# A decoder block on one core: gate and up products ahead of down products, earlier exponentials, a sixth shared block, another order at the end

## The chip, the cores and the metric

The kernel runs on one core of a Trainium2 chip. The metric is device time in microseconds for one execution of the whole program; lower is better. Three runs of the kernel before gave 692.03, 692.99 and 694.44 us, so the median is 692.99.

## The reference

One layer over 256 tokens of width 1024, all in float32. Its parts, cut to what matters here:

```python
c_act = silu(c)
mod = c_act @ w_ada + b_ada                    # (1, 6 * 1024): six vectors
sh1, sc1, g1, sh2, sc2, g2 = split(mod, 6)
h = rmsnorm(x, norm1_g) * (1 + sc1) + sh1
...                                            # one input projection, two attention branches, gates
x = x + g1 * (merged @ w_out)
h2 = rmsnorm(x, norm2_g) * (1 + sc2) + sh2
# mixture of experts: best of 4 groups, best 2 of its 8 experts, 32 experts in all
g_w, g_idx = top_k(softmax(h2 @ w_group + b_group), 1)
e_w, e_idx = top_k(softmax(logits of that group), 2); e_w /= sum(e_w)
y = sum over the two picks of g_w * e_w * ((silu(h2 @ w_gate[e]) * (h2 @ w_up[e])) @ w_down[e])
x = x + g2 * y
out = rmsnorm(x, final_g)
```

The weights are some 257 MB, of which the 32 experts are 201 MB; each weight is read once.

## The kernel before, in words

**Memory and the order of loads.** On-chip memory is one arena, handed out by the program itself while it is written (`Arena`, first fit; `get` with `high` takes the top of the smallest region that fits). A list `order` (lines 187 to 207) holds every weight load in the order in which SP issues it: blocks of w_in and w_ada, the output projections, then for each expert its gate and up weights ("gu") and its down weights ("dn"). `feed()` (line 212) issues the next loads as long as the arena has room, after first serving the areas asked for by `want`. `done(u)` gives an area back and is followed by `feed()`. SP works in order, so a load that waits for its room holds every load behind it. Experts 0 to 4 are loaded in pieces of a quarter ("gu", four of them) and a half ("dn"), later experts whole.

**The order of work.** Inside a `manual_schedule` block the engines named run their instructions as written; outside it a scheduler orders each engine's instructions at build time, and may also put later ones into gaps of a manual block.

**The modulation.** The first two vectors of mod are made ahead of the rest; the other four are eight blocks of 512 columns, numbered 4 to 11, each from two loads. `ada_four(u)` (line 413) either multiplies all eight row groups on TensorE, four at a time in four column strips (line 424), or, for a block in SHARED, lets VectorE add up five of the eight row groups beforehand (`ada_step`, lines 404 to 411, called between the weight splits of the input projection that UNITS pairs the block with, line 547) and multiplies the remaining four on TensorE (line 419). Block 5 belongs to input projection 3 and block 8 to input projection 5.

**The chain to expert 0.** After the output projection the new x is normed and routed in a manual block (lines 947 to 1346): `route` finds group and experts, `places` counts the slots of each token, `first_hots` and `first_sums` gather the rows of expert 0, `gather_first` turns and modulates them (VectorE lines 1052 and 1061, TensorE line 1057), `one_hots` prepares the selection for experts 1 to 3. `first_rows` (line 1233) adds x to the result y in PSUM, where the experts' results are added too; three of its eight products stand inside the block (line 1332) and five behind it (lines 1376 and 1377).

**The experts.** For each expert `hidden(e)` (line 1141) multiplies the gathered rows by gate and up (line 1129 for experts 0 to 4, line 1151 after), and `swiglu` finishes on ScalarE and VectorE; `outputs(e)` (line 1159) multiplies by the down weights (line 1133). Every four experts form a batch: `gather` (line 1018) selects, turns and modulates 128 rows with TensorE (lines 1027 and 1031), and `combine` adds the batch to y. `pick_weights` (line 1243) makes the weights of the picks from the logits with exponentials. After `outputs(0)` come the five products of `first_rows`, the gather of experts 1 to 3 and `pick_weights`.

**The end.** Experts 28 to 31 are added to y one by one (`add`, line 1097: VectorE scales, TensorE adds, line 1104). Expert 31's products come before expert 30's down products, with three warm-up products (`warm`, line 327: bf16 products of a matrix of ones, whose result nobody reads) in the middle. Then `last_outputs` (line 1185) takes the squares of y on ScalarE (line 1216), multiplies y by the final weight on VectorE (`with_g`, line 1210), forms the norm (`power` and `newton`, lines 1198 to 1207) and scales and stores the result. [...]

Of the kernel before, what the change touches and what calls it, by code (L numbers as in the profile page):

```python
# [32 lines left out]
OV_AT = NE - 3  # L33
EXTRAS_AT = 2
UNITS = ((4, (4,)), (3, (5,)), (5, (8,)), (6, (9, 6)), (7, (7,)), (8, (10,)), (9, (11,)))
SHARED = (8, 9, 7, 10, 11)
DMA_SCRATCH = 1024

PLACES = {"x": 25, "xH": 24, "xL": 23, "xn": 22, "xT": 21, "hT": 20, "wsp0": 14,
# [77 lines left out]
def tile_block(ctx: ExitStack, tc: tile.TileContext, d, out):  # L117
# [822 lines left out]
    def places(t):  # L940
# [3 lines left out]
            te.matmul(pos[:, t, :], oneb, mt[:, 0, :], start=False, stop=False)  # L944
        te.matmul(pos[:, t, :], trib, mt[:, t, :], start=False, stop=True)

    chain = ExitStack()
    chain.enter_context(tc.manual_schedule(engines={mybir.EngineType.PE, mybir.EngineType.DVE,
                                                    mybir.EngineType.Activation, mybir.EngineType.Pool}))
# [40 lines left out]
    class Batch:  # L990
# [106 lines left out]
        def add(self, i, dn):  # L1097

            q = self.dq[:, 256 * i:256 * i + 256]
            ve.tensor_tensor(q, dn[:, 0:256], g2g[0], op=OP.mult)  # L1100
            for t in range(2):
                for j in range(4):
                    r = slice(32 * j, 32 * j + 32)
                    te.matmul(y[j // 2][:, j % 2, t, :], self.pt4[r, i, 128 * t:128 * t + 128], q[r, :],  # L1104
                              start=False, stop=i == 3, skip_group_check=True)
# [79 lines left out]
    def last_outputs(hq, b):  # L1185

        e = NE - 1
        m3, ss3 = rt([2], "m3"), rt([2, 2], "ss3")
        q3, u3, r3 = rt([2], "q3"), rt([2], "u3"), rt([2], "r3")
        dn = wk(f"dn{e}")  # L1190
        for i, (k0, n) in enumerate(LAST):
            w = got[("dn", e, i)]
            for k in range(n):
                down(dn, hq, w[:, k, :], k0 + k)
        b.add(3, dn)
        halves = [slice(512 * n, 512 * n + 512) for n in range(2)]

        def power(t):

            i = slice(t, t + 1)  # L1200
            ve.scalar_tensor_tensor(m3[:, i], ss3[:, t, 0:1], EPS * D, ss3[:, t, 1:2], op0=OP.add, op1=OP.add)  # L1201
            gp.tensor_tensor(q3[:, i], m3[:, i], nhalf, op=OP.pow)  # L1202

        def newton(t):
            i = slice(t, t + 1)
            ve.scalar_tensor_tensor(u3[:, i], q3[:, i], m3[:, i], q3[:, i], op0=OP.mult, op1=OP.mult)  # L1206
            ve.scalar_tensor_tensor(r3[:, i], u3[:, i], -3.0, q3[:, i], op0=OP.add, op1=OP.mult)  # L1207

        def with_g(t, n):
            ve.tensor_tensor(v3(fo[:, t, halves[n]], 2), y[n][:, :, t, :], v3(fg[:, halves[n]], 2),  # L1210
                             op=OP.mult)


        for n in (1, 0):
            for t in range(2):
                sc.activation(v3(junk[:, 0:512], 2), y[n][:, :, t, :], AF.Square, accum_out=ss3[:, t, n:n + 1])  # L1216
        with_g(0, 0)
        with_g(1, 0)
        with_g(0, 1)
        power(0)  # L1220
        with_g(1, 1)
        power(1)
        newton(0)
        newton(1)
        for t, n in ((0, 0), (0, 1), (1, 0), (1, 1)):
            o = fo[:, t, halves[n]]
            if t == 1:
                ve.tensor_scalar(o, o, r3[:, t:t + 1], None, op0=OP.mult)  # L1228
            else:
                sc.activation(o, o, AF.Copy, scale=r3[:, t:t + 1])  # L1230
            sp.dma_start(out[0, 128 * t:128 * t + 128, halves[n]], o)

    def first_rows(t, js):
        for j in js:
            te.matmul(y[j // 2][:, j % 2, t, :], ident, x_sb[:, t, 256 * j:256 * j + 256],
                      start=t == 0, stop=False, skip_group_check=True)


    wts = rt([2, 2], "wts")
    gw = rt([2, 1], "gw")  # L1240
    nmx = rt([2, 1], "nmx")

    def pick_weights():
        ve.tensor_scalar(nmx, g8[:, :, 0:1], -1.0, None, op0=OP.mult)
        for t in range(2):
            sc.activation(rt([4], f"gx{t}"), lg[:, t, 0:4], AF.Exp, bias=nmx[:, t, :], accum_out=gw[:, t, :])
        ve.tensor_tensor(wts[:, :, 1:2], v8[:, :, 1:2], v8[:, :, 0:1], op=OP.subtract)
        sc.activation(wts[:, :, 1:2], wts[:, :, 1:2], AF.Exp)
        ve.scalar_tensor_tensor(wts[:, :, 0:1], wts[:, :, 1:2], 1.0, gw, op0=OP.add, op1=OP.mult)
        ve.reciprocal(wts[:, :, 0:1], wts[:, :, 0:1])  # L1250
        ve.tensor_tensor(wts[:, :, 1:2], wts[:, :, 1:2], wts[:, :, 0:1], op=OP.mult)

# [79 lines left out]
    p = wk("xr0")  # L1334
    cur.first_sums(p, 0)
    places(1)
    cur.first_hots(1)
    cur.first_sums(p, 1)
    cur.gather_first(p, modr)
# [3 lines left out]
                                    op0=OP.is_equal, op1=OP.mult, accum_out=ms[:, t, i:i + 1])  # L1343
    cur.one_hots(slice(0, 128))
    cur.ready = 128
    chain.close()
    nxt = None
    for e in range(NE):
        if e % 4 == 0 and e >= 4:
# [5 lines left out]
        if e == NE - 4:  # L1355
# [8 lines left out]
                              start=True, stop=True, skip_group_check=True)  # L1364
                ve.tensor_scalar(fg[:, 512 * n:512 * n + 512], q, -16.0, None, op0=OP.mult)
            cur.weights()
        hq = hidden(e, cur)
        if e == NE - 2:
            with tc.manual_schedule(engines={mybir.EngineType.PE, mybir.EngineType.DVE, mybir.EngineType.Activation}):
                hq, hl = hidden(NE - 1, cur), hq  # L1370
                outputs(e, cur, hl)
                last_outputs(hq, cur)
            break
        outputs(e, cur, hq)
        if e == 0:
            first_rows(0, (3,))
            first_rows(1, range(4))
            cur.gather(slice(32, 128))
            pick_weights()
        if e == 4:  # L1380
            overflow_rows()
        if e % 4 == 0 and e < NE - 4:
# [38 lines left out]
```

## Time and profile before

| | |
|---|---|
| runs | 694.44, 692.03, 692.99 us; median 692.99 |
| profiled execution | 694.41 us; span from first to last instruction 692.6 us |
| mean granted TensorE clock | 0.918 of full speed |
| TensorE busy | 543.2 us, 78% |
| VectorE busy | 297.5 us, 43% |
| ScalarE busy | 157.7 us, 23% |
| DMA | 259.26 MB, mean 374 GB/s over the span |

Times in the profile count from the first instruction. Busy time is an average over stages with different limits, so the table alone doesn't say what bounds the kernel: the slices of the page, the timelines and the windows below do. In a timeline a row gives start and duration in us, engine, line, operation, tile written <- tiles read, shape and count, and in brackets the idle time before it and what ended it. [...]

### The profile page before, as it was taken

The page shows a single profiled execution, that of the slowest core. Times are in us where ns is not written, and L with a number is a line of the kernel's source. Part 1 is how long each engine was busy: PE and PEld are TensorE (multiplying, and loading weights), DVE is VectorE, ACT ScalarE, POOL GpSimd, SP SyncE. Part 2 cuts the span into 40 slices and gives each one's busy share as a digit, 9 for nine tenths or more (in the row PEclk, how much of TensorE's full clock was granted, in tenths as well). Part 3 has the DMA queues.
Part 4 walks back from the last instruction along what each step waited for, and adds up shares of the span by engine and source line. Part 5 has one row for each costly group of instructions (what it writes and reads, how often), then busy time and mean ns, then how long its engine had stood idle before and what let it go on. Part 6 is the DMA issues. An engine that isn't in the chain of part 4 may idle for free. (4 is left out here: it accounts for less than half of the span.)

```text
span 692.6 us, 14947 instructions
## 1 busy us (share of the span) xinstructions
PE 543.2 (78%) x6499; PEld 379.8 (55%) x6499; DVE 297.5 (43%) x840; ACT 157.7 (23%) x350; POOL 6.7 (1%) x21
## 2 busy tenths in 40 slices
PE   8999999999999997878848647656855755686572
PEld 4667766666788744556635435434544444365451
DVE  5359977858787466454314213121421211221012
ACT  3345755575554321001000000000000000010002
POOL 1000000000000000000000000000000000000000
PEclk9999999999999999999988989976998998799775
DMA  9999979649986989999999999999999999999971
GB/s 316 365 374 386 387 253 387 223 155 387 409 324 225 341 297 399 427 429 423 428 427 423 427 429 424 425 428 427 425 428 427 424 424 429 426 425 428 425 308 61
DMA packets 53965, 259.26 MB, mean 374 GB/s; under 512 B 5297, under 2 KB 13706, under 8 KB 42250
## 3 DMA queue, kind: packets, MB, share of 16 engines
q1 hardware_dynamic: 53802, 258.26, 93.1%
q8 instruction: 52, 0.85, 0.5%
q14 instruction: 15, 0.12, 0.0%
q10 hardware_dynamic: 96, 0.03, 0.0%
HBM read 257.23 MB, written 1.05 MB: 373 GB/s over the span
## 5 line engine op out<-in xcount | busy, mean ns | idle before, releaser
L1151 PE MATMUL gu<-gu,xe 128*32 128x128 f32 x3456 | 121.8, 303 | 53.1 <-DMA gu<-in_w_up_dram 28.7
L1151 PEld LDWEIGHTS gu<-gu,xe 128*32 128x32 f32 x3456 | 107.6, 122 | 68.3 <-DMA gu<-in_w_up_dram 33.3
L1133 PE MATMUL dn<-dn,hq 128*32 128x256 f32 x1024 | 79.7, 462 | 67.5 <-DMA dn<-in_w_down_dram 45.1
L1133 PEld LDWEIGHTS dn<-dn,hq 128*32 128x32 f32 x1024 | 39.9, 127 | 98.5 <-issue 65.0
L1139 DVE TENSOR_TENSOR dq<-dn,g2g 32x256 f32<-32x256 f32 x112 | 47.1, 420 | 96.4 <-PE dn L1133 94.9
L1121 DVE TENSOR_TENSOR hid<-hid,gu 128x128 f32<-128x128 f32 x32 | 9.2, 287 | 170.5 <-ACT hid L1120 170.5
L1120 ACT ACTIVATE hid<-gu 128x128 f32<-128x128 f32 x32 | 8.9, 278 | 280.2 <-PE gu L1151 250.8
L521 PE MATMUL in<-win,xH 128*128 128x512 f32 x112 | 45.5, 408 | 0.0
L520 PE MATMUL in<-win,xL 128*128 128x512 f32 x112 | 45.5, 406 | 0.0
L519 PE MATMUL in<-win,xH 128*128 128x512 f32 x112 | 45.1, 403 | 0.0
L509 DVE TENSOR_TENSOR win<-win,win 128x512 fp32r<-128x512 f32 x56 | 37.3, 686 | 7.4 <-ACT win L508 7.2
L508 ACT ACTIVATE win<-win 128x512 fp32r<-128x512 f32 x56 | 33.8, 628 | 15.4 <-PE in L521 10.1
L1027 PE MATMUL xr<-x,pr 128*128 128x512 f32 x64 | 31.6, 638 | 0.0
L1094 PE MATMUL y<-dq,pt 128*128 128x256 f32 x112 | 26.8, 393 | 2.7 <-DVE dq L1139 2.7
L519 PEld LDWEIGHTS in<-win,xH 128*128 128x128 f32 x112 | 21.1, 188 | 8.4 <-issue 2.9
L1094 PEld LDWEIGHTS y<-dq,pt 128*128 128x128 f32 x112 | 19.9, 193 | 9.8 <-DVE dq L1139 7.9
L521 PEld LDWEIGHTS in<-win,xH 128*128 128x128 f32 x112 | 21.1, 188 | 6.8 <-issue 3.2
L1034 DVE TENSOR_SCALAR xe<-xe,modP 128x128 f32<-128x128 f32 (+1 forms) x64 | 20.9, 398 | 9.0 <-PE xe L1031 9.0
L520 PEld LDWEIGHTS in<-win,xL 128*128 128x128 f32 x112 | 21.1, 189 | 6.1 <-issue 2.4
L1028 ACT ACTIVATE rows<-xr 128x512 f32<-128x512 f32 x16 | 9.6, 597 | 61.3 <-PE xr L1027 61.3
L1027 PEld LDWEIGHTS xr<-x,pr 128*128 128x128 f32 x64 | 12.4, 205 | 17.1 <-issue 17.1
L568 DVE TENSOR_TENSOR wq<-winq,wq 128x1024 fp32r<-128x1024 f32 x12 | 14.2, 1220 | 12.8 <-ACT wq L565 12.8
(359 smaller groups left out, 724.0 us busy)
## 6 DMA issues: line engine op xcount, KB each, us to landing
gu<-in_w_gate_dram SPq DMA_DIRECT2D x27, 2048.0 KB, 39.3
gu<-in_w_up_dram SPq DMA_DIRECT2D x27, 2048.0 KB, 39.1
dn<-in_w_down_dram SPq DMA_DIRECT2D x26, 2048.0 KB, 39.1
ada<-in_w_ada_dram SPq DMA_DIRECT2D x16, 1024.0 KB, 12.3
win<-in_w_in_dram SPq DMA_DIRECT2D x14, 1024.0 KB, 12.9
gu<-in_w_gate_dram SPq DMA_DIRECT2D x20, 512.0 KB
gu<-in_w_up_dram SPq DMA_DIRECT2D x20, 512.0 KB, 9.0
dn<-in_w_down_dram SPq DMA_DIRECT2D x10, 1024.0 KB, 8.8
```

Source lines behind the costliest of these rows:

```text
L508: sc.activation(wh, w[:, k0:k0 + n, :], AF.Copy)
L509: ve.tensor_sub(wl, w[:, k0:k0 + n, :], wh.bitcast(F32))
L519: te.matmul(acc[t], lh[:, k0 + k, s], wh[:, k, :], start=k0 + k == 0, stop=False)
L520: te.matmul(acc[t], ll[:, k0 + k, s], wh[:, k, :], start=False, stop=False)
L521: te.matmul(acc[t], lh[:, k0 + k, s], wl[:, k, :], start=False, stop=last and k == n - 1)
L568: ve.tensor_sub(wq[u][:, 1], got[("winq", u, q)], wq[u][:, 0].bitcast(F32))
L1027: te.matmul(p[0:w, :], self.pr[:, t, 0:w], x_sb[:, t, 512 * g:512 * g + 512], start=t == 0, stop=t == 1)
L1034: ve.tensor_scalar(self.xe[:, k, s], q[k // 4][:, o + s.start:o + w], modP[:, 0, k:k + 1], modP[:, 1, k:k + 1], op0=OP.mult, op1=OP.add)
L1094: te.matmul(y[j // 2][:, j % 2, t, :], self.pt[rows, 128 * t:128 * t + 128], self.dq[rows, 256 * j:256 * j + 256], start=False, stop=False ...
L1133: te.matmul(dn[32 * j:32 * j + 32, 0:256], hq[:, 32 * k:32 * k + 32], w[:, 256 * j:256 * j + 256], start=k == 0, stop=k == 3)
L1139: ve.tensor_tensor(dq[s, 256 * j:256 * j + 256], dn[r, 0:256], g2g[0][r, :], op=OP.mult)
L1151: te.matmul(gu[32 * j:32 * j + 32, 128 * q:128 * q + 128], b.xe[:, k, s], w[:, k, 128 * j:128 * j + 128], start=k == 0, stop=k == KC - 1)
```

## The change

It puts block 5 of the modulation into SHARED. It moves the exponentials of the picks into the chain, behind `places(1)`, with a Silu of one column behind them, and the rest of the picks' weights behind `one_hots`. The manual block now reaches over expert 0's gate and up products, the gather of experts 1 to 3 and the five products of `first_rows`, which stand in that order and ahead of expert 0's down products. For experts 2 and 3 the gate and up products are written ahead of the down products of experts 1 and 2. At the end eight warm-up products stand between expert 31's gate and up products and expert 30's down products, two more in `add` for the last two experts, and the squares of half 0 come behind the first two products with the final weight.

```diff
--- before.py
+++ after.py
@@ -33,7 +33,8 @@
 OV_AT = NE - 3
 EXTRAS_AT = 2
 UNITS = ((4, (4,)), (3, (5,)), (5, (8,)), (6, (9, 6)), (7, (7,)), (8, (10,)), (9, (11,)))
-SHARED = (8, 9, 7, 10, 11)
+SHARED = (5, 8, 9, 7, 10, 11)
+AHEAD = 3
 DMA_SCRATCH = 1024
 
 PLACES = {"x": 25, "xH": 24, "xL": 23, "xn": 22, "xT": 21, "hT": 20, "wsp0": 14,
@@ -944,6 +945,26 @@
             te.matmul(pos[:, t, :], oneb, mt[:, 0, :], start=False, stop=False)
         te.matmul(pos[:, t, :], trib, mt[:, t, :], start=False, stop=True)
 
+
+    wts = rt([2, 2], "wts")
+    gw = rt([2, 1], "gw")
+    nmx = rt([2, 1], "nmx")
+
+    def pick_powers():
+        ve.tensor_scalar(nmx, g8[:, :, 0:1], -1.0, None, op0=OP.mult)
+        ve.tensor_tensor(wts[:, :, 1:2], v8[:, :, 1:2], v8[:, :, 0:1], op=OP.subtract)
+        gx = rt([4], "gx")
+        for t in range(2):
+            sc.activation(gx, lg[:, t, 0:4], AF.Exp, bias=nmx[:, t, :], accum_out=gw[:, t, :])
+        sc.activation(wts[:, :, 1:2], wts[:, :, 1:2], AF.Exp)
+
+        sc.activation(gx[:, 0:1], nhalf, AF.Silu)
+
+    def pick_weights():
+        ve.scalar_tensor_tensor(wts[:, :, 0:1], wts[:, :, 1:2], 1.0, gw, op0=OP.add, op1=OP.mult)
+        ve.reciprocal(wts[:, :, 0:1], wts[:, :, 0:1])
+        ve.tensor_tensor(wts[:, :, 1:2], wts[:, :, 1:2], wts[:, :, 0:1], op=OP.mult)
+
     chain = ExitStack()
     chain.enter_context(tc.manual_schedule(engines={mybir.EngineType.PE, mybir.EngineType.DVE,
                                                     mybir.EngineType.Activation, mybir.EngineType.Pool}))
@@ -1098,6 +1119,8 @@
 
             q = self.dq[:, 256 * i:256 * i + 256]
             ve.tensor_tensor(q, dn[:, 0:256], g2g[0], op=OP.mult)
+            if i >= 2:
+                warm(2, wk(f"warm{i}"))
             for t in range(2):
                 for j in range(4):
                     r = slice(32 * j, 32 * j + 32)
@@ -1211,11 +1234,14 @@
                              op=OP.mult)
 
 
-        for n in (1, 0):
+        def squares(n):
             for t in range(2):
                 sc.activation(v3(junk[:, 0:512], 2), y[n][:, :, t, :], AF.Square, accum_out=ss3[:, t, n:n + 1])
+
+        squares(1)
         with_g(0, 0)
         with_g(1, 0)
+        squares(0)
         with_g(0, 1)
         power(0)
         with_g(1, 1)
@@ -1234,21 +1260,6 @@
         for j in js:
             te.matmul(y[j // 2][:, j % 2, t, :], ident, x_sb[:, t, 256 * j:256 * j + 256],
                       start=t == 0, stop=False, skip_group_check=True)
-
-
-    wts = rt([2, 2], "wts")
-    gw = rt([2, 1], "gw")
-    nmx = rt([2, 1], "nmx")
-
-    def pick_weights():
-        ve.tensor_scalar(nmx, g8[:, :, 0:1], -1.0, None, op0=OP.mult)
-        for t in range(2):
-            sc.activation(rt([4], f"gx{t}"), lg[:, t, 0:4], AF.Exp, bias=nmx[:, t, :], accum_out=gw[:, t, :])
-        ve.tensor_tensor(wts[:, :, 1:2], v8[:, :, 1:2], v8[:, :, 0:1], op=OP.subtract)
-        sc.activation(wts[:, :, 1:2], wts[:, :, 1:2], AF.Exp)
-        ve.scalar_tensor_tensor(wts[:, :, 0:1], wts[:, :, 1:2], 1.0, gw, op0=OP.add, op1=OP.mult)
-        ve.reciprocal(wts[:, :, 0:1], wts[:, :, 0:1])
-        ve.tensor_tensor(wts[:, :, 1:2], wts[:, :, 1:2], wts[:, :, 0:1], op=OP.mult)
 
 
 
@@ -1334,6 +1345,7 @@
     p = wk("xr0")
     cur.first_sums(p, 0)
     places(1)
+    pick_powers()
     cur.first_hots(1)
     cur.first_sums(p, 1)
     cur.gather_first(p, modr)
@@ -1343,7 +1355,7 @@
                                     op0=OP.is_equal, op1=OP.mult, accum_out=ms[:, t, i:i + 1])
     cur.one_hots(slice(0, 128))
     cur.ready = 128
-    chain.close()
+    pick_weights()
     nxt = None
     for e in range(NE):
         if e % 4 == 0 and e >= 4:
@@ -1364,19 +1376,26 @@
                               start=True, stop=True, skip_group_check=True)
                 ve.tensor_scalar(fg[:, 512 * n:512 * n + 512], q, -16.0, None, op0=OP.mult)
             cur.weights()
-        hq = hidden(e, cur)
+
+        if e == 0:
+            hq = hidden(0, cur)
+            cur.gather(slice(32, 128))
+            first_rows(0, (3,))
+            first_rows(1, range(4))
+            chain.close()
+        elif e == 1 or e > AHEAD:
+            hq = hidden(e, cur)
+        hl = hq
+        if 0 < e < AHEAD:
+            hq = hidden(e + 1, cur)
         if e == NE - 2:
             with tc.manual_schedule(engines={mybir.EngineType.PE, mybir.EngineType.DVE, mybir.EngineType.Activation}):
                 hq, hl = hidden(NE - 1, cur), hq
+                warm(8, wk("warm1"))
                 outputs(e, cur, hl)
                 last_outputs(hq, cur)
             break
-        outputs(e, cur, hq)
-        if e == 0:
-            first_rows(0, (3,))
-            first_rows(1, range(4))
-            cur.gather(slice(32, 128))
-            pick_weights()
+        outputs(e, cur, hl)
         if e == 4:
             overflow_rows()
         if e % 4 == 0 and e < NE - 4:
```

## Rows read from the trace of the kernel before

**Rows 1.** The page, part 2: busy tenths of TensorE, DMA rate, in 40 slices

```profile
PE   8999999999999997878848647656855755686572
...
GB/s 316 365 374 386 387 253 387 223 155 387 409 324 225 341 297 399 427 429 423 428 427 423 427 429 424 425 428 427 425 428 427 424 424 429 426 425 428 425 308 61
```

**Rows 2.** Timeline of TensorE: an unshared block (L424), then a shared one (L419)

```profile
105.19 1.93 PE L424 MATMUL ada<-ada,ccol 128*32 128x512 f32 x16
...
115.85 0.63 PE L419 MATMUL ada<-ada,ccol 128*32 128x512 f32 x3
...
116.30 0.61 PE L419 MATMUL ada<-ada,ccol 128*32 128x512 f32 x3
```

**Rows 3.** Groups of VectorE by form, 60 to 130 us: a step of sharing

```profile
L411 DVE SCALAR_TENSOR_TENSOR ada<-ada,ccol 128x512 f32<-128x512 f32 x9 | 6.7, 750 | 0.1
```

**Rows 4.** Timeline of VectorE: idle time behind the steps of a shared block

```profile
98.51 1.17 DVE L437 SCALAR_TENSOR_TENSOR part<-brow,part 1x128 f32<-1x128 f32 x4 [3.31 <-ACT part L428]
```

**Rows 5.** Timeline of TensorE, 246 to 250 us: up to expert 0's first products

```profile
246.08 1.11 PE L1235 MATMUL y<-x,ident 128*128 128x256 f32 x4
...
247.12 1.10 PE L1045 MATMUL xr<-x,pr 128*32 128x256 f32 x8
...
249.68 0.59 PE L1235 MATMUL y<-x,ident 128*128 128x256 f32 x2
...
250.20 3.66 PE L1129 MATMUL gu<-gu,xe 128*32 128x256 f32 x64
```

**Rows 6.** Timeline of VectorE, 246 to 250 us: what two of those wait for

```profile
246.35 0.30 DVE L1039 TENSOR_SCALAR pr<-slots,pos_ps,mr 128x32 f32<-128x32 f32 x1 [1.00 <-PE pos_ps L945]
...
249.44 0.42 DVE L1061 TENSOR_TENSOR xe<-xs,modP 128x256 f32<-128x256 f32 x1 [0.73 <-PE xs L1057]
```

**Rows 7.** Timeline of TensorE: expert 0's down products, then the two parts of the gather

```profile
256.35 1.93 PE L1133 MATMUL dn<-dn,hq 128*32 128x256 f32 x32 [1.38 <-DVE hq L1124]
...
258.21 3.70 PE L1027 MATMUL xr<-x,pr 128*128 128x512 f32 x8
...
262.60 1.16 PE L1031 MATMUL xe<-ident,rows 128*128 128x128 f32 x8 [0.69 <-ACT rows L1028]
```

**Rows 8.** Timeline of SP's queue: loads of expert 4, gate and up, then down

```profile
251.33 0.33 SPq L241 DMA_DIRECT2D gu<-in_w_gate_dram  x1
...
258.34 7.02 SPq L250 DMA_DIRECT2D dn<-in_w_down_dram  x2
```

**Rows 9.** Windows: us, busy time of PE, PEld, DVE, ACT, POOL; clock, DMA share, GB/s

```profile
252.00:253.00 1.00, 1.00 (x24) 0.60 (x20) 1.00 (x8) 0.00 (x0) 0.00 (x0) 1.00 0.55 82
...
250.00:260.00 10.00, 8.62 (x120) 4.57 (x119) 6.57 (x31) 1.56 (x2) 0.00 (x0) 1.00 0.77 251
```

**Rows 10.** Timeline of TensorE at the end: down products, warm-up, the adds to y

```profile
645.96 1.93 PE L1133 MATMUL dn<-dn,hq 128*32 128x256 f32 x32 [1.47 <-SPq L1296]
...
663.84 0.82 PE L330 MATMUL warm<-oneb 128*128 128x512 bf16 x3
...
670.42 2.60 PE L1133 MATMUL dn<-dn,hq 128*32 128x256 f32 x32 [3.01 <-SPq L1296]
...
673.55 2.09 PE L1104 MATMUL y<-dq,pt 32*128 32x256 f32 x16 [0.52 <-DVE dq L1100]
...
675.57 3.29 PE L1133 MATMUL dn<-dn,hq 128*32 128x256 f32 x32
...
679.42 1.15 PE L1104 MATMUL y<-dq,pt 32*128 32x256 f32 x16 [0.56 <-DVE dq L1100]
```

**Rows 11.** Windows of half a microsecond: the granted clock at the end

```profile
672.00:672.50 0.50, 0.50 (x12) 0.14 (x4) 0.00 (x0) 0.00 (x0) 0.00 (x0) 0.50 0.48 205
```

**Rows 12.** Timeline of the end: squares on ScalarE, products and sums on VectorE

```profile
680.65 0.60 ACT L1216 ACTIVATE tail<-y 128x512 f32<-128x512 f32 x1 [12.85 <-PE y L1104]
...
683.53 1.89 DVE L1210 TENSOR_TENSOR fo<-y,tail 128x512 f32<-128x512 f32 x3 [4.17 <-ACT tail L1216]
...
686.01 0.15 DVE L1201 SCALAR_TENSOR_TENSOR m<-ss 128x1 f32<-128x1 f32 x1
```

## The prediction

> **What bounds the kernel now.** I read the page's slices first: TensorE is at 9 tenths until slice 14, the DMA rate has holes in slices 5 to 14 and then stands at about 427 GB/s to the end of slice 37 [rows 1]. So there are two regimes. Until some 250 us TensorE paces the kernel: the holes are loads that wait for memory that TensorE has not yet released. After that the weight stream paces it, since TensorE only waits for arrivals. The join is expert 0: its gate and up products start at 250.20 [rows 5], and as their quarters finish, SP issues expert 4's loads, the first at 251.33 [rows 8]. The DMA had run dry before: the window from 250 to 260 us moved 251 GB/s [rows 9]. Whatever makes expert 0's products start earlier moves the stream and the end with it; whatever leaves a hole in the stream behind that point is lost. The third part is the end, where the last weights have landed and a chain of TensorE, ScalarE and VectorE remains [rows 10 to 12].
>
> **The change, part by part.**
>
> *Sharing block 5.* A block that is not shared is sixteen matmul instructions in 1.93 us; a shared one is eight, from 115.85 to 116.30 + 0.61 = 116.91, so 1.06 us [rows 2]. Removed: 1.93 - 1.06 = 0.87 us of TensorE, on the path, as TensorE is full there [rows 1]. Added: five VectorE steps, at most 5 x 0.75 = 3.75 us [rows 3], in front of weight splits that TensorE needs. What hides them is idle VectorE time of 3.31 us just behind the steps of block 8 [rows 4], which can slide into it; without that cover up to 3.75 us of splits would be late. I take the 0.44 us that does not fit as hidden by the depth of the split buffers. Gain 0.9, bounds 0.9 and -2.9. The order in which the two loads of block 5 are released is the old one, so SP's queue is untouched.
>
> *The five products of first_rows leave the chain.* Before, the scheduler put them into gaps in front of expert 0, and two of them overran. The sums of the second token tile could start when VectorE was done at 246.35 + 0.30 = 246.65, but a filler from 246.08 held them until 247.12: 0.47. Expert 0's operand was ready at 249.44 + 0.42 = 249.86, but a filler from 249.68 held the products until 250.20: 0.34 [rows 5, 6]. Some 0.05 of each is handover, so 0.7 is gained. The fillers now come, in written order, behind the gather. Gain 0.7, bounds 0 (others are scheduled in) and 0.8.
>
> *Exponentials of the picks early.* Three exponentials, a dummy Silu and two short VectorE operations move ahead of the second set of one-hots. VectorE sat idle 1.00 us there [rows 6], which takes the two; ScalarE has the time until expert 0's SwiGLU. The table of Silu is then in place sooner, but the gather now runs during that SwiGLU, so nothing waits for it. Cost 0; if the cover fails, expert 0's down product, which waited 1.38 us for its operand before [rows 7], has the gather's 5.55 us in front of it all the same.
>
> *Gather and first_rows ahead of expert 0's down product.* This has a price. From the start of expert 0's products: 3.5 us for themselves [rows 5], 263.76 - 258.21 = 5.55 for the gather [rows 7], ten instructions of first_rows at (1.11 - 0.14) / 4 = 0.24 each, 2.4 [rows 5], and 1.9 for the down product [rows 7]: 13.35 us, against 258.2 - 250.2 = 8.0 before. SP may load the first half of expert 4's down weights only into room that this product frees, and its queue is in order, so all later loads stand behind it. When does the stream run dry? Expert 4's gate and up weights are 4.19 MB by their shapes. Of the 2.51 MB moved from 250 to 260 us [rows 9] the last 1.66 us carry 0.71 at 427 GB/s, so by 258.34 [rows 8] 1.80 have gone, and 2.39 last 5.6 us more, to 263.9, or 13.7 after the products' start. The next issue falls at 13.35 + 0.1, and data flow about 1.1 us behind an issue (issue 251.33, engines half busy in the window from 252 to 253 [rows 8, 9]): at 14.55. Idle 0.85, and with a slow restart 1.1 us lost. Bounds: 0 if the down product slips in earlier, 4.1 if the restart is as poor as in the window of 251 GB/s, (427 - 251) / 427 x 10. I take 1.1 by the sum of rows.
>
> *Experts 2 and 3 ahead.* The products of expert 2 run while expert 1's SwiGLU does, which saves TensorE waits like the 1.38 [rows 7]. I followed the allocator through the new order of releases: expert 5's up weights wait for the third quarter of expert 2 instead of its first, expert 5's down and expert 6's gate weights for expert 1's down product, and from expert 7 on each load has the trigger it had. Once the stream is full TensorE waits for data, so this gives 0; it refills the queue behind the dry spot. Stream in all: -0.9 - 0.7 + 1.1 = -0.5.
>
> *Warm-up products at the end.* Expert 30's down products took 2.60 us, the add 2.09, expert 31's down products 3.29; the same work took 1.93, 1.15 and 1.93 elsewhere [rows 10]. [...] I take 2.9; bounds 0 and 3.0.
>
> *Squares reordered.* Four squares in a row end at 683.53, four products follow, and the last sum is taken at 686.01 [rows 12]. In the new order the products of half 0 run beside the squares of half 1, and the reverse. The last square still ends at about 683.5, the fourth product at about 683.6, the last sum follows at 683.7: 2.3 gained. No row here shows both engines reading PSUM at the end, so the lower bound is 0, the upper 2.4.
> [...]
>
> **The sum.** -0.5 - 2.9 - 2.3 = -5.7. The profiled execution took 694.41 us (span 692.6 and 1.8 around it), so 688.7; it is the slowest of three, and from the median of 692.99 I predict 687.3.
>
> **The rivals.**
> 1. *No dry spot.* The down product gets into the 0.69 us gap of the gather [rows 7] or the scheduler lets it pass. For it: the gap; against: first_rows is written ahead. 687.3 - 1.1 = 686.2. Chance 0.20.
> 2. *The clock falls all the same.* The stretches at the end stay a string of short bursts and waits [rows 10]; against it: eight warm-ups leave under 1 us of the 3.01 idle. 687.3 + 2.9 = 690.2. Chance 0.15.
> [...]
> 3. *Slower.* The place is the scheduler's choice behind the gather: if the products of experts 1, 2 and 3, whose weights have landed, go ahead of expert 0's down product, SP's queue stands for 3 x 3.66 us [rows 5] more: 687.3 + 11.0 = 698.3. It decides the sign from 5.7 us of idle stream on. Against it: before, the down product was not overtaken even while TensorE idled 1.38 us [rows 7]. Chance 0.04.
> 4. *The order does not come about.* Outside the hand-ordered stretch the scheduler may still place expert 1's down product before expert 2's products. Then the loads of experts 5 and 6 come a little later, 0.3 at most where the queue is short: 687.6. Chance 0.10.
>
> **How the numbers follow.** My forecast has 0.51. A measurement here tells a change of about 0.3%, 2.1 us, from none, so faster means under 690.9. Nearly all of the forecast (0.48), all of rival 1 (0.20), half of rival 2 (0.08) and most of rival 4 (0.09) lie there: 0.85. Rival 3 is slower: 0.04. The rest is 0.11. Range: the best terms together (stream -1.6, end -3.0 and -2.4) give 686.0, and a little recovered stream 685.0; the clock lost with one more microsecond of dry stream gives 691.0.
>
> **What would show it.** Right: expert 0's products start near 248.6; one thin spot near 262; 0.50 gone from the clock at 672; ScalarE's squares and VectorE's products side by side; the last sum about 2.3 us sooner after the last add. Wrong: a window of several microseconds without DMA after 262, a down product of 3.3 us at the end, or products that still wait for the last square.

## The result, and the profile after

The changed kernel takes 689.18 us (median of 5 runs, 688.74 to 689.96) against 692.99 for the kernel before (5 runs, 692.03 to 694.44): a ratio of 0.9942, 95% interval 0.9928 to 0.9956, so about 4.0 us faster. The profiled execution took 689.18 us with a span of 687.0, against 694.41 and 692.6 before.

The page's slices of the changed kernel (busy tenths of TensorE, DMA rate), against [rows 1]:

```profile
PE   8999999999999999977757767755775675568564
GB/s 317 365 374 387 387 252 387 245 172 388 412 314 247 337 263 388 429 425 426 425 426 428 425 426 427 426 427 425 425 424 428 425 429 426 426 425 427 425 376 104
```

The two regimes are as before: a full TensorE with holes in the DMA rate, then a steady stream of some 427 GB/s. The second vector instruction of the routing, its first maximum (MAX8), tells how far the first regime has got. The timeline of VectorE has it for the kernel before and, below, for the changed one:

```profile
239.85 0.17 DVE L927 MAX8 g<-lg 128x8 f32<-128x8 f32 x1
```

```profile
237.20 0.17 DVE L928 MAX8 g<-lg 128x8 f32<-128x8 f32 x1
```

That is 2.65 us sooner, where the sharing of block 5 was to give 0.9. From there to expert 0, the timeline of TensorE in the changed kernel, which answers to [rows 5, 7]:

```profile
238.24 1.08 PE L874 MATMUL lg<-wge,x2T 128*128 128x40 f32 x8 [0.75 <-ACT x2T L881]
...
240.03 0.18 PE L946 MATMUL pos_ps<-mt,trib 128*128 128x32 bf16 x1 [0.60 <-DVE mt L939]
...
240.93 2.93 PE L1261 MATMUL y<-x,ident 128*128 128x256 f32 x6
...
248.30 3.66 PE L1152 MATMUL gu<-gu,xe 128*32 128x256 f32 x64
251.89 3.70 PE L1048 MATMUL xr<-x,pr 128*128 128x512 f32 x8
...
257.28 2.32 PE L1261 MATMUL y<-x,ident 128*128 128x256 f32 x10
...
260.00 1.93 PE L1156 MATMUL dn<-dn,hq 128*32 128x256 f32 x32
...
262.22 7.11 PE L1152 MATMUL gu<-gu,xe 128*32 128x256 f32 x128
```

Expert 0's products start at 248.30 instead of 250.20, and the written order came about: gather, ten instructions of `first_rows`, expert 0's down product, then 128 products of experts 1 and 2 in one row. The six products of `first_rows` in the chain are new to the argument: 2.93 us here, 1.56 in the profile before. The windows say why (columns as in [rows 9], the granted clock is the third number from the end):

```profile
240.00:241.00 1.00, 0.97 (x18) 0.48 (x17) 0.86 (x6) 0.29 (x1) 0.00 (x0) 0.71 0.98 340
241.00:242.00 1.00, 1.00 (x3) 0.82 (x4) 0.90 (x7) 0.38 (x1) 0.00 (x0) 0.50 1.01 344
...
250.00:260.00 10.00, 9.31 (x83) 5.53 (x75) 6.85 (x28) 1.47 (x3) 0.00 (x0) 1.00 0.86 279
...
262.00:263.00 1.00, 1.00 (x18) 0.58 (x21) 0.97 (x3) 0.38 (x1) 0.00 (x0) 1.00 1.09 369
263.00:264.00 1.00, 1.00 (x28) 0.57 (x24) 0.95 (x4) 0.00 (x0) 0.00 (x0) 1.00 0.83 258
264.00:265.00 1.00, 1.00 (x24) 0.62 (x20) 1.00 (x6) 0.00 (x0) 0.00 (x0) 1.00 0.97 381
```

After waits of 0.75 and 0.60 us the clock fell to 0.50; in the profile before it had stayed at 1.00 from 236 to 250 us. The last three rows are the thin spot: against 427 GB/s they miss 0.14 + 0.40 + 0.11 = 0.65 us of stream. The end of the changed kernel, TensorE, ScalarE and VectorE in one timeline, against [rows 10, 12]:

```profile
666.99 1.90 PE L331 MATMUL warm<-oneb 128*128 128x512 bf16 x8
...
670.05 2.19 PE L1156 MATMUL dn<-dn,hq 128*32 128x256 f32 x32 [1.17 <-SPq L1307]
...
672.76 1.15 PE L1127 MATMUL y<-dq,pt 32*128 32x256 f32 x16
673.84 1.93 PE L1156 MATMUL dn<-dn,hq 128*32 128x256 f32 x32
...
676.32 1.15 PE L1127 MATMUL y<-dq,pt 32*128 32x256 f32 x16
677.50 1.29 DVE L1233 TENSOR_TENSOR fo<-y,tail 128x512 f32<-128x512 f32 x2 [1.23 <-PE y L1127]
677.56 0.60 ACT L1239 ACTIVATE tail<-y 128x512 f32<-128x512 f32 x1 [10.11 <-PE y L1127]
...
680.44 0.16 DVE L1224 SCALAR_TENSOR_TENSOR m<-ss 128x1 f32<-128x1 f32 x1
```

The granted clock is 1.00 from the first of these down products to the last add, in every window of one microsecond from 670 to 678 us (that the first of them takes 2.19 us instead of 1.93 is not the clock's doing and stays open), and products and squares run side by side (677.50 and 677.56). From expert 30's down product to the first square it takes 7.51 us instead of 10.23, from there to the last sum 2.88 instead of 5.36.

### The profile page after: what moved, and what is told of

It is laid out like the page before. It is cut to its first block, busy times and chain, and to the rows that moved or that the text cites. A ratio compares the mean times of both kernels' runs of the same rounds, so it can differ in the third digit from the quotient of the medians.

```text
span 687.0 us, 14970 instructions
## 1 busy us (share of the span) xinstructions
PE 547.4 (80%) x6503; PEld 380.6 (55%) x6503; DVE 300.8 (44%) x845; ACT 157.8 (23%) x351; POOL 6.7 (1%) x21
## 5 line engine op out<-in xcount | busy, mean ns | idle before, releaser
L1174 PEld LDWEIGHTS gu<-gu,xe 128*32 128x32 f32 x3456 | 105.9, 121 | 65.4 <-DMA gu<-in_w_up_dram 33.8
L1156 PE MATMUL dn<-dn,hq 128*32 128x256 f32 x1024 | 84.3, 482 | 65.0 <-DMA dn<-in_w_down_dram 51.0
L1156 PEld LDWEIGHTS dn<-dn,hq 128*32 128x32 f32 x1024 | 42.0, 132 | 96.3 <-issue 73.7
```

Source lines behind the costliest of these rows:

```text
L1156: te.matmul(dn[32 * j:32 * j + 32, 0:256], hq[:, 32 * k:32 * k + 32], w[:, 256 * j:256 * j + 256], start=k == 0, stop=k == 3)
L1174: te.matmul(gu[32 * j:32 * j + 32, 128 * q:128 * q + 128], b.xe[:, k, s], w[:, k, 128 * j:128 * j + 128], start=k == 0, stop=k == KC - 1)
```

## The experiments

The kernels of one group below ran on one chip together with fresh runs of the kernel before, and each ratio is against those. Three more columns come from the timeline of each profile: where expert 0's products start, where expert 30's down product starts (how far the stream has got), and the time from there to the end of the last scaling of the output (the end alone).

| run | median, us | ratio, 95% | expert 0 | expert 30 | end alone |
|---|---|---|---|---|---|
| before, first profile | 692.99 | | 250.20 | 670.42 | 17.73 |
| changed, first profile | 689.18 | 0.9942, 0.9928 to 0.9956 | 248.30 | 670.05 | 12.54 |
| e1_end_only | 691.15 | 0.9953, 0.9935 to 0.9971 | 251.93 | 672.84 | 12.30 |
| e2_no_end | 691.67 | 0.9968, 0.9953 to 0.9982 | 248.65 | 670.07 | 16.25 |
| e3_no_squares | 691.14 | 0.9951, 0.9935 to 0.9967 | 248.19 | 669.53 | 14.89 |
| e4_no_warm | 690.59 | 0.9937, 0.9915 to 0.9959 | 248.29 | 670.19 | 13.90 |
| r1_changed_again | 688.38 | 0.9912, 0.9888 to 0.9935 | 247.81 | 668.85 | 12.55 |
| e5_not_shared | 691.08 | 0.9950, 0.9930 to 0.9970 | 250.16 | 671.90 | 12.41 |
| e6_old_order | 688.08 | 0.9906, 0.9884 to 0.9927 | 248.74 | 669.55 | 12.40 |
| e8_down_first | 688.95 | 0.9919, 0.9895 to 0.9944 | 248.69 | 669.92 | 12.42 |
| e11_share_only | 692.27 | 0.9984, 0.9968 to 1.0 | 248.57 | 669.58 | 16.41 |
| e9_chain_warm | 687.72 | 0.9910, 0.9887 to 0.9932 | 246.83 | 669.04 | 12.51 |
| e12_old_order_warm | 686.82 | 0.9898, 0.9875 to 0.9921 | 247.28 | 668.21 | 12.41 |
| r2_before_again | 694.68, one run | | 252.32 | 673.57 | 14.87 |

The kernel before had medians of 693.74 (e1 to e4), 694.58 (r1, e5, e6, e8) and 693.68 us (the last four).

### The end, taken apart

e1 is the kernel before with the three edits of the end. e2 is the changed kernel without them, e3 without the order of the squares, e4 without the warm-up products.

The order of the squares in e2 and e3:

```diff
         squares(1)
+        squares(0)
         with_g(0, 0)
         with_g(1, 0)
-        squares(0)
         with_g(0, 1)
```

The warm-up products in e2 and e4:

```diff
-            if i >= 2:
-                warm(2, wk(f"warm{i}"))
...
-                warm(8, wk("warm1"))
```

> The kernel before with only the three edits of the end: eight warm-up products, two more in each of the last two adds, squares reordered. In the two profiles the stretch from expert 30's down products to the last add fell from 10.21 us (670.42 to 680.63) to 7.45 us (670.05 to 677.50), and from there to the second sum of squares from 5.38 to 2.94. Theory 1 (the end gives all it showed, the rest about nothing): 5.2 us less than before, ratio 0.9925, so better than the whole change. Theory 2 (the end gives 5.2 and the rest costs 1.4, which is why the medians differ by only 3.8): the same ratio, 0.9925; the next kernel tells it from theory 1. Theory 3 (the clock at the end falls in the profiled execution of before but not in most, so the end gives 2.4 for the squares and about 1.4 for the clock): ratio 0.9945.

> The changed kernel with the end of the kernel before. Theory 1 (stream ahead by 0.7 us, as the bytes moved by 300 us show): 0.4 to 0.7 us less than before, ratio 0.999. Theory 2 (the new order costs 1.4 us in most executions): ratio 1.002. Theory 3: no difference, ratio 0.9995 to 1.0. [...]

> The changed kernel with the squares in the old order. All theories: 2.4 us more than the changed kernel, ratio to before 0.9942 + 0.0035 = 0.998, and in the profile the products with the final weight wait for the last square again, with 5.4 us from the last add to the second sum. If ScalarE and VectorE slowed each other in the changed kernel the difference is under 2.4.

> The changed kernel without the warm-up products of the end. Theories 1 and 2: 2.8 us more than the changed kernel, ratio to before 0.998, with expert 31's down products at 3.3 us. Theory 3: 1.4 us more, ratio 0.996, as the clock falls in only some executions. If the warm-ups did nothing for the clock: 0.

In the profile the squares behave as forecast. With warm-ups the end takes 12.44 us on the mean of eight profiles (12.30 to 12.55), and 14.89 in e3, so their order is worth 2.45. The timeline of e3 has the products behind the last square again, where the changed kernel has them beside it:

```profile
676.92 0.60 ACT L1239 ACTIVATE tail<-y 128x512 f32<-128x512 f32 x1 [10.00 <-PE y L1127]
...
679.80 1.89 DVE L1233 TENSOR_TENSOR fo<-y,tail 128x512 f32<-128x512 f32 x3 [4.17 <-ACT tail L1239]
...
682.27 0.15 DVE L1224 SCALAR_TENSOR_TENSOR m<-ss 128x1 f32<-128x1 f32 x1
```

The warm-ups are another matter. Without them the end loses 13.90 - 12.44 = 1.46 in e4, and not at the places of the profile before: one down product takes 3.52 us, and the products behind it 1.15 and 1.93, as in the changed kernel at a granted clock of 1.00 (timeline of e4):

```profile
670.19 3.52 PE L1154 MATMUL dn<-dn,hq 128*32 128x256 f32 x32 [2.98 <-SPq L1305]
...
674.26 1.15 PE L1125 MATMUL y<-dq,pt 32*128 32x256 f32 x16 [0.54 <-DVE dq L1121]
675.34 1.93 PE L1154 MATMUL dn<-dn,hq 128*32 128x256 f32 x32
```

Of the four ratios that were expected here only one came: e1's 0.9953 agrees with theory 3 (0.9945) and not with 0.9925. e2 (0.9968), e3 (0.9951) and e4 (0.9937) all came out lower than every theory had them (0.999 or more, 0.998, and 0.996 or more), except for the rival of e4 that the warm-ups do nothing. All were reckoned from the changed kernel's first ratio, 0.9942. From the 0.9912 of r1, below, the squares would make 0.9947 and theory 3's 1.4 us for the warm-ups 0.9932, both inside the intervals. So the time alone doesn't tell e4 from the changed kernel; what the warm-ups are worth rests on the profiles.

### The kernel before, a second time

> The kernel before once more, for a second profile. Theory that its first profile was one of two kinds: here the granted clock falls in the routing chain as in the others, the six products of the first sums take 2.5 to 2.9 us, and from the last down product but one to the first square it takes 8.5 to 9.5 us instead of 10.2. Rival: both stretches repeat (1.56 and 10.2 us).

The theory holds for the chain and more than holds for the end. Same instructions, same waits, and the clock is granted elsewhere: it is 0.50 from 242 to 248 us, where the first profile has 1.00, and 1.00 from 664 to 682 us, where the first has 0.50 from 672 to 678 (timeline of TensorE of this second profile of the kernel before):

```profile
243.83 2.93 PE L1235 MATMUL y<-x,ident 128*128 128x256 f32 x6
...
252.32 3.66 PE L1129 MATMUL gu<-gu,xe 128*32 128x256 f32 x64
...
673.57 1.93 PE L1133 MATMUL dn<-dn,hq 128*32 128x256 f32 x32 [3.01 <-SPq L1296]
676.04 1.15 PE L1104 MATMUL y<-dq,pt 32*128 32x256 f32 x16 [0.54 <-DVE dq L1100]
677.24 1.93 PE L1133 MATMUL dn<-dn,hq 128*32 128x256 f32 x32
```

The six products take 2.93 us instead of 1.56, expert 0 starts at 252.32 instead of 250.20, and the stream is 3.15 us later at expert 30 (673.57 against 670.42). The end then loses nothing: it idles the same 3.01 us, yet the products take 1.93, and the end is 14.87 us long. Its first part, from the down product to the first square, takes 7.38 us, where I had expected 8.5 to 9.5 and the first profile has 10.23. Both executions take 694.4 to 694.7 us, one having lost its clock at the end, the other in the chain. Against the 14.89 us that e3, with warm-ups and the old squares, needs for its end, the clock thus cost 2.84 us in the first profile, nothing in this one and 1.36 in e2 (16.25).

### The sharing of block 5

e5 takes it out of the changed kernel, e11 puts it alone into the kernel before; r1 is the changed kernel once more, beside e5.

```diff
-SHARED = (5, 8, 9, 7, 10, 11)
+SHARED = (8, 9, 7, 10, 11)
```

> The changed kernel once more, beside the next three. Theory 1 as it now stands (the two halves add up: the rest alone came to 0.9968 of before, the end alone to 0.9953): 0.9921, 5.5 us less. If they overlap: 0.9942 as in the first measurement. [...]

> The changed kernel with block 5 no longer shared. As forecast (0.87 us of TensorE): ratio 0.0013 above that of the changed kernel, and the first MAX8 of the routing 0.9 us later than its 237.2. As the two profiles show (2.65 us ahead at the routing, of which this step would be the only cause): 239.8, and up to 2.6 us, 0.0037, more. If VectorE's extra steps cost what they save: no difference.

> The kernel before with block 5 among the shared ones and nothing else. Theory: the second routing maximum comes some 2.5 us sooner (237.2 to 237.4 instead of 239.7 to 239.9), the whole stream behind it keeps 2 to 2.5 us of that, and the time is 2.0 to 2.7 us below the kernel before. Rival, the sum of the prediction: only the removed products count, the maximum comes 0.9 us sooner and the time is 0.9 us lower. Second rival: the gain needs the other parts too (early exponentials, first rows ahead), and the time alone is that of the kernel before within 0.5 us.

In every profile the second instruction of the routing shown above tells which kernel it is: with sharing it is at 237.15 in e11 and 237.20 in the changed kernel. From 90 us to there e11 follows the changed kernel's timeline within 0.05 us, so this edit alone makes the whole lead of 2.6 us at the routing. The starts of expert 30 say the same: 672.18 on the mean of the four profiles without sharing (before, r2, e1, e5), 669.72 on that of the eight with it and without e9's warm-ups, 2.46 sooner. In times, e5 against r1 gives 2.7 us (seven runs of 689.42 to 691.93, six of 686.78 to 689.75); e11 gives only 1.1 (0 to 2.2), though its stream stands at 669.58. Its end takes it back, and mostly not by the clock, which is 1.00 from 664 to 678 us and 0.50 behind that. At 16.41 us it is 1.54 longer than that of r2, as the timeline of TensorE in e11 shows:

```profile
673.25 1.50 PE L1133 MATMUL dn<-dn,hq 128*32 128x256 f32 x24
675.95 0.64 PE L1133 MATMUL dn<-dn,hq 128*32 128x256 f32 x8 [1.20 <-SPq L1296]
```

Expert 31's down product waited 1.20 us for its last quarter of weights. It had not come too early: in r2 it starts as long after expert 30's (3.67 us in both) and waits for nothing. The load was late: in e11 the wait for it ends 6.37 us after expert 30's start, while in the first profiles of both kernels it lands some 4.8 after it (issued at 640.9 before and 640.6 in the changed kernel, 34.3 and 34.2 us to landing). e4 has the same 6.37, in a load of TensorE's weights at 676.56, hidden there behind the slow product; in the other profiles expert 31's down product shows no wait for weights. What delays the load is open, and so is whether e11's other runs have it; if they do, 2.46 - 1.20 = 1.26 is near the measured 1.1.

Where the gain comes from is seen between 84 us and the four quarter sums of block 10, 172.38 in the changed kernel and 175.05 before, where TensorE idles at most 0.8 us at a time in either. First the row groups of TensorE in the kernel before, then in the changed one (the unshared products):

```profile
L424 PE MATMUL ada<-ada,ccol 128*32 128x512 f32 x48 | 5.8, 598 | 0.0
```

```profile
L425 PE MATMUL ada<-ada,ccol 128*32 128x512 f32 x32 | 3.8, 598 | 0.0
```

I added up, over that stretch, the time from each row's start to the next one's. The unshared products fall from 5.57 to 3.70 us: -1.87, one block, as the prediction had it. The shared products, eight more of them, should have risen by 1.0 and rose by 0.05 (5.90 to 5.95). One set of eight had been torn apart in the kernel before by transposes of the attention (timeline of TensorE, before):

```profile
158.35 1.04 PE L419 MATMUL ada<-ada,ccol 128*32 128x512 f32 x2
159.32 0.55 PE L771 MATMUL odt<-ident,ods 128*128 128x128 f32 x3
159.80 0.62 PE L419 MATMUL ada<-ada,ccol 128*32 128x512 f32 x2
...
160.25 0.60 PE L419 MATMUL ada<-ada,ccol 128*32 128x512 f32 x2
```

and stands whole in the changed one:

```profile
157.12 0.63 PE L420 MATMUL ada<-ada,ccol 128*32 128x512 f32 x3
...
157.57 0.60 PE L420 MATMUL ada<-ada,ccol 128*32 128x512 f32 x3
...
158.12 0.50 PE L520 MATMUL in<-win,xH 128*128 128x512 f32 x1
```

The eight instructions take 160.79 - 158.35 - 0.48 = 1.96 us without the transposes before, and 1.00 after. The rest, some 0.7, lies in many places: the transposes of line 771 cost 0.49 less, the other small groups (lines 694, 710 and 635) 0.23 + 0.20 + 0.15 less, the input projection 0.31 more. So 2.6 is 0.9 from fewer products and 1.7 from another interleaving of the same instructions, which the scheduler drew up anew: in e11 nothing else was changed. That it is the tearing itself that costs the 0.96 is read from this one set; no run puts the transposes back by hand.

### The order around expert 0

e6 puts the gather and `first_rows` behind expert 0's down product again and takes the products of experts 2 and 3 back to their places; the early exponentials, sharing and the end stay. e8 only moves the down product ahead of `first_rows`.

```diff
-            hq = hidden(0, cur)
-            cur.gather(slice(32, 128))
-            first_rows(0, (3,))
-            first_rows(1, range(4))
             chain.close()
-        elif e == 1 or e > AHEAD:
-            hq = hidden(e, cur)
-        hl = hq
-        if 0 < e < AHEAD:
-            hq = hidden(e + 1, cur)
+        hq = hl = hidden(e, cur)
...
         outputs(e, cur, hl)
+        if e == 0:
+            first_rows(0, (3,))
+            first_rows(1, range(4))
+            cur.gather(slice(32, 128))
```

The edit of e8:

```diff
             cur.gather(slice(32, 128))
+            outputs(0, cur, hq)
             first_rows(0, (3,))
             first_rows(1, range(4))
             chain.close()
...
-        outputs(e, cur, hl)
+        if e:
+            outputs(e, cur, hl)
```

> The changed kernel with the order of the kernel before: the hand-ordered stretch ends ahead of expert 0, gather and first_rows behind its down products, no expert ahead; the exponentials stay early. Theory 1 (the new order starts expert 0 0.8 us sooner and loses about as much behind it): ratio within 0.0015 of the changed kernel. Theory 2 (the new order starves the stream for more than it gains): this kernel is faster, by up to 1.5 us, and the window from 250 to 270 us moves more. Theory 4 (the fillers kept back are worth more, as without them the chain is free): slower by 1 us or more.

> The changed kernel with expert 0's down products ahead of first_rows, still in the hand-ordered stretch, so the load of expert 4's down weights is issued about 2.4 us sooner, at 259.6 instead of 261.96. If the thin spot behind it (rates of 369, 258 and 381 GB/s from 262 to 265 us, 0.6 us lost) comes from that load: it vanishes and 0.6 us are gained, ratio 0.001 lower. If it is a slow restart from the earlier dry stretch: nothing.

Neither moved the time beyond its noise: ratios of 0.9906 and 0.9919 beside r1's 0.9912, on one chip. The profiles show that this is two effects that cancel, as theory 1 of e6 had it. From expert 0's start to expert 30's (the table) the six profiles with the old order (before, r2, e1, e6, e11, e12) take 420.2 to 421.3 us, 420.9 on the mean; the seven with the new one (all the others but e8) take 421.0 to 422.2, 421.6 on the mean. So the new order loses 0.8 us behind expert 0. It does so at once. The windows have the first 50 us behind expert 0's start, in the changed kernel, in e6 and in e8:

```profile
248.30:298.30 50.00, 47.42 (x688) 29.16 (x688) 30.17 (x115) 4.54 (x11) 0.00 (x0) 1.00 0.94 374
```

```profile
248.74:298.74 50.00, 42.98 (x554) 24.73 (x554) 26.12 (x96) 4.16 (x10) 0.00 (x0) 1.00 0.95 385
```

```profile
248.69:298.69 50.00, 47.42 (x688) 29.32 (x688) 30.18 (x114) 4.54 (x11) 0.00 (x0) 1.00 0.95 380
```

The same window gives 380 to 385 GB/s in the six profiles and 373 to 377 in the seven, 7.4 apart on the mean: 0.37 MB, or 0.9 us at 427 GB/s. SP's queue shows where it goes. In the changed kernel the down weights of expert 4 go out at 261.96, in e6 at 256.33:

```profile
261.96 1.72 SPq L251 DMA_DIRECT2D dn<-in_w_down_dram  x2
```

```profile
256.33 7.03 SPq L251 DMA_DIRECT2D dn<-in_w_down_dram  x2
```

In e6 the pair of issues takes 7.03 us from the first's start to the second's end, so the second half goes out as late as in the changed kernel (the pair ends at 263.36 and 263.68). But the first half is under way by then, and from 262 to 265 us e6 moves 438, 422 and 438 GB/s where the changed kernel has its thin spot. In e8 the pair starts at 260.20, not the expected 259.6, and the spot is gone as well (windows of e8, whose neighbours have 430 and 414 GB/s):

```profile
263.00:264.00 1.00, 1.00 (x27) 0.57 (x23) 0.98 (x5) 0.15 (x1) 0.00 (x0) 1.00 1.04 422
```

So the spot comes from the late issue and not from a slow restart. The 0.6 us that e8 was to gain are too few for its interval (0.9895 to 0.9944) to show. What the new order loses here it gains ahead of expert 0: 0.4 to 0.6 us, by e9 and e12 below and by the first pair of profiles.

### The clock in the chain

Twelve profiles have no warm-ups in the chain, and in eleven the six products take 2.45 to 2.93 us; only the first profile before has 1.56. e9 fills the two waits seen above, e12 does so with the old order of e6.

```diff
     keep_turned(1, p)
+    warm(3, acc[0])
     logits(1, 1)
+    warm(2, acc[0])
```

> The changed kernel with five more warm-up products in the routing chain, three ahead of the second logits and two behind them, where TensorE stood idle for 0.75 and 0.6 us before the granted clock fell to 0.50. Theory: the clock holds, the six products of the first sums take 1.56 instead of 2.5 to 2.9 us, expert 0's products start 0.9 to 1.4 us sooner, and the time is 0.9 to 1.4 us below the changed kernel's. Rival: the products start sooner but the weights' stream does not get ahead (the moved bytes at 270 and 300 us as in the changed kernel within 0.1 MB), and the time is the changed kernel's within 0.4 us. Second rival: the clock falls all the same and nothing moves.

> The changed kernel with the order of the experts and of the first rows as before (as in the run of the old order) and with the same five warm-up products in the routing chain. Theory that the start of expert 0 carries the stream: the six products at 1.56 us, expert 0's products 0.9 to 1.4 us sooner than without, and a time 0.9 to 1.4 us below that of the changed kernel. Rival: the same time as the old order without the warm-up products had beside the changed kernel, within 0.5 us.

The clock held in both: it is 1.00 in every window from 236 to 250 us. Timeline of TensorE in e9:

```profile
239.25 0.60 PE L331 MATMUL wo<-oneb 128*128 128x512 bf16 x2
...
240.13 0.18 PE L946 MATMUL pos_ps<-mt,trib 128*128 128x32 bf16 x1 [0.16 <-DVE mt L939]
...
240.81 1.56 PE L1263 MATMUL y<-x,ident 128*128 128x256 f32 x6
```

Expert 0's products start at 246.83 and 247.28, 1.0 to 1.5 us sooner than in the like kernels r1, the changed one and e6 (247.81, 248.30, 248.74). From the first maximum to there it takes 9.53 us in e9 and 9.94 in e12, both at the full clock: the order alone is worth 0.41 here. Of the earlier start the stream keeps a part at most. By 300 us it has moved 101.26 MB in e9 against 101.02 in r1, but 100.68 in the changed kernel's first profile, so two profiles of one kernel lie further apart; and at expert 30 e9 stands between those two (669.04; 668.85 and 670.05). e12 has 101.41 MB against 101.05 in e6 and is 1.34 us ahead of it at expert 30. The medians, 687.72 and 686.82, are the lowest but one and the lowest of the study, but they come from another chip than r1 and e6, and the ratios say less: 0.9910 beside r1's 0.9912, no gain, and 0.9898 beside e6's 0.9906, some 0.6 us. The intervals overlap. That the clock can be held in the chain is shown; that it pays in time is not.

## Why the prediction was right, and where it was not

The sign and the range held: 689.18 lies in 685.0 to 691.0, 1.9 above the forecast of 687.3. By its steps:

- **Sharing block 5** ("Gain 0.9"): mis-sized. It is worth 2.6 us at the routing and 2.5 at expert 30. The removed products are counted rightly (0.87); the step left out that the scheduler orders the whole stretch anew, with TensorE full, so that a set of products torn or whole counts on the path at once. The VectorE steps cost nothing that shows, as argued; the bound below (2.9 slower) was far too cautious, the one above (0.9) was no bound.
- **`first_rows` out of the chain** ("Gain 0.7"): in the pair of profiles expert 0 came 1.90 sooner = 2.65 of sharing - 1.37 of clock + 0.62, so 0.6 is left for this step; e9 against e12 gives 0.41. Right in mechanism, a little large.
- **Exponentials early** (0): right, but for less than was thought: the scheduler had already placed the exponentials there, the first at 244.28 us before and 244.34 after, though they were written behind `outputs(0)`. What moved is the load of Silu's table, from 253.96 to 245.26 us; by e6, where expert 0's down product waits 0.40 us instead of 1.38, that helps the old order. The step was not tried by itself.
- **The dry spot** ("I take 1.1"): right in place and cause. The spot is there, at 262 to 265; the down product ended 13.6 us after expert 0's start, forecast 13.35; and the spot is gone in e6 and e8, where that load goes out sooner. By the windows it costs 0.65 us, against the old order 0.8 to 0.9, so the 1.1, with its allowance for a slow restart, is a little large.
- **Experts 2 and 3 ahead** (0): with the gather and `first_rows`, within the noise by e6; by itself it was not tried.
- **Warm-ups** ("I take 2.9"): mis-sized by taking one execution for all. No run shows the 2.9: it was my estimate from rows 10, (2.60 - 1.93) + (2.09 - 1.15) + (3.29 - 1.93) = 2.97 less 0.1. The pair of profiles gives 10.23 - 7.51 = 2.72, but over the five profiles without warm-ups the clock cost 2.84, 0, 1.36, 1.46 (e4, by its product of 3.52 us) and, in e11 without its wait for weights, at most 0.3: a mean of 1.2. The upper bound was this one profile; the lower one, 0, is what r2 showed.
- **Squares** (2.3): 2.45 by e3, 2.48 by the pair. No row of the kernel before shows ScalarE and VectorE reading y side by side, so the overlap was my estimate. The rows at 677.50 and 677.56 show it: VectorE reads half 0 of y (`y[0]`) while ScalarE reads half 1 (`y[1]`), and neither is slower for it (a square 0.60 us, two products 1.29; before, a square 0.60 and three products 1.89).

The two errors of size, 1.6 too little for sharing and 1.7 too much for the warm-ups, offset each other, and that they did is luck: with the sizes of the runs the sum is -2.5 - 0.6 + 0.8 - 1.2 - 2.45 = -5.95, against the -5.7 predicted. Of the ten ratios without chain warm-ups eight hold the matching sum in their intervals (e5: 3.45 by the sum, 3.5 measured; r1: 5.95 and 6.1; e2: 2.3 and 2.2). Two come out lower: e11, perhaps by its wait, and the first comparison, with 4.0 (3.1 to 5.0), though r1's interval of 4.5 to 7.8 meets it. Some 0.4 of what is missing there lies outside the span (689.18 - 687.0 = 2.2 us around it, 1.8 before), but r1 has the same 2.2. The rest stays open.

Of the rivals, 1 (no dry spot) fell with the row at 263. 2 (the clock falls all the same at the end) fell: the nine profiles with the warm-ups have down products of 1.93 to 2.20 us there, and the windows of the changed kernel, e9 and e12 have a granted clock of 1.00. In the chain, for which I had not forecast it, the clock did fall: its mean from 240 to 250 us is 0.66 to 0.84 in eleven of the twelve profiles without warm-ups there, and 1.00 in the first profile before. 3 (slower, expert 0's down product overtaken) and 4 (the order does not come about) fell with the rows from 251.89 to 262.22.

## What to carry to other kernels

Where one engine is full and a scheduler orders its work, removing a piece is worth its own time plus or minus what the new interleaving does, and the second can be the larger (here 0.9 and 1.7 us): bound it by the pieces seen torn in the profile, on both sides. A clock lost in one profile is a draw, not a constant (here 2.84 and 0 us at the end of one kernel): before a fix is priced at what it cost there, a second profile of the same kernel tells how often it is lost, and whether a loss at one place only stands for one at another. And a time that doesn't move can be two terms that cancel: each is to be measured from the event where the two part, here the start of expert 0, and not from the start of the kernel.

## What the runs showed that I had not expected

The granted clock differs between executions of one program at the same instruction: at 242 to 243 us of the kernel before it was 1.00 in one profile and 0.50 in the other, after the same busy shares (0.25 and 1.00 of the two microseconds ahead). The second row is of the second profile:

```profile
242.00:243.00 1.00, 0.41 (x10) 0.31 (x13) 0.90 (x5) 0.32 (x2) 0.00 (x0) 1.00 1.06 389
```

```profile
242.00:243.00 1.00, 0.68 (x8) 0.48 (x11) 0.90 (x5) 0.29 (x1) 0.00 (x0) 0.50 1.05 369
```

What sets the point at which it changes was not shown. The first profile's 2.84 us should have been priced as one draw of several.

The transfers also restart slowly: after the dry stretch around 250 us the changed kernel moved 279 GB/s from 250 to 260 us though SP had issued its first load at 249.43, and e11, in the old order, had moved even less by 260 us (83.91 MB against 84.10). Issues that took SP 0.4 us elsewhere took up to 1.4 us there, in the changed kernel, 1.9 in e11 and 0.8 before. What makes them longer was not tried.
